# Two-layer trunk on one core: bulk work of GpSimd handed to VectorE and ScalarE, ALiBi slopes folded into the queries, the score products of two heads issued in turn, a product of the state-space part widened

## The chip, the cores and the metric

The kernel runs on one core of one Trainium2 chip. The metric is the device time of one execution in microseconds; the median of several executions counts. The engines are called as in the profile: PE (TensorE's matmuls), PEld (its weight loads), DVE (VectorE), ACT (ScalarE), POOL (GpSimd), SP (SyncE, which here issues the loads of the weights).

## The reference, cut to what matters

A sequence of 256 tokens of width 1024, in float32, goes through two layers. Each layer is a mixer and a feed-forward part. The mixer of layer 0 is a state-space mixer (S5, 48 groups of 16 channels, 64 states each), that of layer 1 is causal attention of 12 heads with ALiBi; beside both runs an attention of 4 heads into 256 memory tokens.

```python
for i in range(2):
    h = rmsnorm(x, g)
    z = h @ w_in[i]                       # the mixer's input and the memory queries
    mixed = s5(z[..., :768]) if i == 0 else moba(q, k, v, slopes)
    mem = softmax(mq @ mk.T / 8) @ mv     # 4 heads of 64, 256 memory tokens
    x = x + concat(mixed, mem) @ w_out[i]
    h = rmsnorm(x, g_ffn)
    x = x + (silu(h @ w_gate) * (h @ w_up)) @ w_down

def s5(u):                                # a: complex decay, b, c: complex maps, one per group
    bu = einsum('bsgc,gpc->bsgp', u, b)
    xs = scan(xs * a + bu)                # over the 256 tokens
    y  = einsum(real(xs), c_re) - einsum(imag(xs), c_im) + d * u
    y  = gelu(y)
    return y * sigmoid(y @ w_glu + b_glu)

def moba(q, k, v, slopes):                # with 256 tokens: plain causal attention
    s = q @ k.T / 8 - slopes[h] * (t - t')     # masked where t' > t
    return softmax(s) @ v
```

## The kernel before

**Products.** PE multiplies in a reduced float32 type (fp32r), so each operand is split in two: `hi` is the value rounded to that type and `lo` is the rest. A product is three matmuls, hi·hi, hi·lo and lo·hi, in `mm3` (L192, L193, L194). Weights arrive by DMA as 128x1024 tiles `raw` (a ring of four buffers); `split_hi` (L150) makes `whi` on ACT and `split_lo` (L168) makes `wlo` on DVE or on POOL. A table of two letters for each weight tile (`ENGINES0`, `ENGINES1`) decides that: "ag" is ACT and POOL, "av" is ACT and DVE. In the feed-forward parts all are "av". Activations are split likewise (L272 on ACT, L273 on DVE).

**Order.** The mixers are written as named steps, and two lists (`ORDER0`, `ORDER1`) set the order in which the steps are issued; within one engine that order stays. In `ORDER1`, `s4` is the scores of head 4, `x4` its exponentials, `n4` the normalisation, `t4` the transposition, `h4` the hi and lo halves of the probabilities, `p4` the product with the values, `o4` the output; `qp2`, `kp2` are the projections of a pair of heads, `qe2`, `ke2` their evacuation and splitting, and `a4` the ALiBi bias. Heads 0 to 3 are the memory's, 4 to 15 the causal ones.

**State-space part.** The 48 groups are worked in six units of eight. For each unit, `s5_ab` (L587 to L589) and `s5_wo` (L599 to L601) form the matrices `AB` and `wo` out of products `tA` and `tB`, of which half are made on POOL (L588, L599); `s5_angles` makes angles, cosines, sines and the decay `dec` (L627, POOL); `s5_tm` (L641) multiplies `AB` and `wo`, 32 columns of `AB` at a time; the scan is L691; `s5_turn` (L695 on POOL, L696 on DVE) turns the scan's result `Z` by the angles, and L704 to L706 multiply it out. Beside it stand the memory's keys and values: their row norms go through Newton steps on 128x2 tiles (L236 to L242), `diag` (L250), and the value tile `mv` (L298 on ACT, L299 on DVE), from which PE goes on at L190.

**Attention.** `alibi` (L958) makes `sb = -slope * dist` on POOL. `h_scores` multiplies a head's queries and keys, which sit on 64 of PE's 128 rows, an even head on the lower and an odd one on the upper half (L351 for the block that is partly masked, L192 to L194 for the other); all matmuls of a head are issued together. `h_exp` adds the scores to `sb` and takes the maximum (L364 on DVE, from PSUM and SBUF), negates it (L366) and exponentiates (L370 on ACT). `h_norm` takes the reciprocal of the sum (L376) and multiplies the probabilities by it (L378 on DVE, twice a head, from SBUF to SBUF).

Of the kernel before, what the change touches and what calls it, by code (L numbers as in the profile page):

```python
# [89 lines left out]
class Trunk:  # L90
# [29 lines left out]
    def plan(self, name, idx, shape, eng="av"):  # L120

        self.chunks.append((name, idx, shape, eng))

    def load_w(self, n=1, parts=1, between=None):
        for _ in range(n):
            if self.n_load < self.stop:
                name, idx, (a, b), eng = self.chunks[self.n_load]
# [8 lines left out]
                self.loaded.append((raw, b, eng))  # L136

    def split_hi(self):
        nc = self.nc
# [4 lines left out]
        raw, b, eng = self.loaded.pop(0)
        if eng == "":
            self.half.append((raw, None, b, eng))
            return
# [1 line left out]
        if eng[0] == "a":
            nc.scalar.activation(out=hi, in_=raw, func=AF.Copy)  # L150
        else:
            nc.gpsimd.tensor_scalar(hi, raw, 1.0, 0.0, op0=ALU.mult, op1=ALU.add)
        self.half.append((raw, hi, b, eng))

    def split_lo(self):
# [4 lines left out]
        raw, hi, b, eng = self.half.pop(0)  # L160
# [141 lines left out]
    def qk_evac(self, pool, ps, r, nm, bufs, keep=False):  # L302
# [14 lines left out]
    def mem_heads(self, out):  # L317
        hs = []
        for pr in range(2):
            for e in range(2):  # L320
# [3 lines left out]
                hs.append(h)  # L324
        return hs

    def moba_heads(self, p, q, k, vt, out):
        hs = []
        for e in range(2):
# [3 lines left out]
            hs.append(h)  # L333
        return hs

    def h_scores(self, h):
# [4 lines left out]
        h.s = s = self.bank("sc")  # L341
        if h.slope is None:
            h.blocks = [(0, slice(0, T)), (1, slice(T, 2 * T))]
            h.order, h.n0 = [0, 2, 1, 3], 0
            for i, c in h.blocks:
                t = slice(i * P, (i + 1) * P)
                self.mm3(s[:, c], [(qh[r, t], ql[r, t])], [(kh[r], kl[r])])
        else:
            h.blocks = [(0, slice(0, P)), (1, slice(P, P + T))]
            h.order, h.n0 = [0, 1, 2], P  # L350
            mm(s[:, 0:P], qf[r, 0:P], kf[r, 0:P], start=True, stop=True)  # L351
            self.mm3(s[:, P:P + T], [(qh[r, P:T], ql[r, P:T])], [(kh[r], kl[r])])
# [985 lines left out]
```

## Time and profile before

| | |
|---|---|
| executions | 646.88, 647.16, 649.87 us; median 647.16 us |
| profiled execution | 649.4 us, span 647.6 us |
| mean granted clock of TensorE in it | 0.978 of full speed |
| busy in the span | PE 95%, PEld 90%, DVE 71%, ACT 56%, POOL 15% |
| DMA | mean 163 GB/s, 105.8 MB |

The span runs from the first to the last instruction of the profiled execution; 1.8 us of its time lie outside. PE counts as busy while a matmul is under way, at whatever clock, so a busy PE is not yet one that could not be faster.

### The profile page before, as it was taken

The page shows a single profiled execution, that of the slowest core. Times are in us where ns is not written, and L with a number is a line of the kernel's source. Part 1 is how long each engine was busy: PE and PEld are TensorE (multiplying, and loading weights), DVE is VectorE, ACT ScalarE, POOL GpSimd, SP SyncE. Part 2 cuts the span into 40 slices and gives each one's busy share as a digit, 9 for nine tenths or more (in the row PEclk, how much of TensorE's full clock was granted, in tenths as well). Part 3 has the DMA queues.
Part 4 walks back from the last instruction along what each step waited for, and adds up shares of the span by engine and source line. Part 5 has one row for each costly group of instructions (what it writes and reads, how often), then busy time and mean ns, then how long its engine had stood idle before and what let it go on. Part 6 is the DMA issues. An engine that isn't in the chain of part 4 may idle for free. (4 is left out here: it accounts for less than half of the span.)

```text
span 647.6 us, 12327 instructions
## 1 busy us (share of the span) xinstructions
PE 615.9 (95%) x4808; PEld 585.3 (90%) x4808; DVE 462.0 (71%) x858; ACT 364.0 (56%) x651; POOL 94.0 (15%) x76
## 2 busy tenths in 40 slices
PE   6998889899999999999999999989999999999995
PEld 6877769789999999999999899979999999998884
DVE  7979767679766666666646999978776666664444
ACT  7584826668555555554444758746655555553333
POOL 2435531110000000000036522211000000000001
PEclk9999979899999999999999999979999999999998
DMA  7564231445655565556665334425555655555511
GB/s 216 173 192 117 66 97 50 155 172 185 206 194 192 194 191 193 190 189 182 203 196 184 124 106 156 131 97 167 194 193 192 194 193 194 193 177 181 187 55 66
DMA packets 35578, 105.82 MB, mean 163 GB/s; under 512 B 4032, under 2 KB 9280, under 8 KB 35520
## 3 DMA queue, kind: packets, MB, share of 16 engines
q1 hardware_dynamic: 35520, 105.03, 50.3%
q8 instruction: 38, 0.62, 0.4%
q14 instruction: 20, 0.16, 0.1%
HBM read 102.40 MB, written 1.05 MB: 160 GB/s over the span
## 5 line engine op out<-in xcount | busy, mean ns | idle before, releaser
L150 ACT ACTIVATE whi<-raw 128x1024 fp32r<-128x1024 f32 (+2 forms) x176 | 183.3, 1043 | 151.9 <-PE mm L193 105.6
L168 DVE TENSOR_TENSOR wlo<-raw,whi 128x1024 fp32r<-128x1024 f32 (+1 forms) x157 | 190.0, 1210 | 49.2 <-PE mm L1119 28.3
L168 POOL TENSOR_TENSOR wlo<-raw,whi 128x1024 fp32r<-128x1024 f32 (+2 forms) x19 | 44.8, 2363 | 240.7 <-PE mm L194 208.6
L1057 DVE TENSOR_TENSOR gu<-mm,rr 128x512 f32<-128x512 f32 x44 | 30.4, 692 | 51.4 <-PE mm L194 50.7
L192 PE MATMUL mm<-hh,whi 128*128 128x256 f32 x176 | 48.6, 276 | 0.0
L193 PE MATMUL mm<-hl,whi 128*128 128x256 f32 x176 | 48.6, 276 | 0.0
L194 PE MATMUL mm<-hh,wlo 128*128 128x256 f32 x176 | 48.6, 276 | 0.0
L272 ACT ACTIVATE hh<-ev 128x256 fp32r<-128x256 f32 x44 | 18.3, 419 | 36.7 <-DVE ev L1049 36.7
L192 PEld LDWEIGHTS mm<-hh,whi 128*128 128x128 f32 x176 | 33.0, 188 | 0.0
L193 PEld LDWEIGHTS mm<-hl,whi 128*128 128x128 f32 x176 | 33.0, 188 | 0.0
L194 PEld LDWEIGHTS mm<-hh,wlo 128*128 128x128 f32 x176 | 33.0, 188 | 0.0
L273 DVE TENSOR_TENSOR hl<-ev,hh 128x256 fp32r<-128x256 f32 x44 | 18.7, 425 | 19.7 <-ACT hh L272 19.6
L1146 POOL TENSOR_TENSOR o<-xt,gf 128x256 f32<-128x256 f32 (+1 forms) x3 | 2.8, 921 | 196.7 <-issue 193.3
L192 PE MATMUL mm<-xg0h,whi 128*128 128x256 f32 x102 | 29.8, 292 | 0.0
L193 PE MATMUL mm<-xg7l,whi 128*128 128x256 f32 x102 | 28.4, 278 | 1.1 <-DVE xg7l L268 1.1
L192 PE MATMUL mm<-xg7h,whi 128*128 128x256 f32 x102 | 28.3, 277 | 0.0
L193 PE MATMUL mm<-xg0l,whi 128*128 128x256 f32 x102 | 28.2, 277 | 0.0
L192 PE MATMUL mm<-xg1h,whi 128*128 128x256 f32 x102 | 28.2, 277 | 0.0
L194 PE MATMUL mm<-xg0h,wlo 128*128 128x256 f32 x102 | 28.2, 277 | 0.0
L194 PE MATMUL mm<-xg1h,wlo 128*128 128x256 f32 x102 | 28.2, 277 | 0.0
L193 PE MATMUL mm<-xg1l,whi 128*128 128x256 f32 x102 | 28.2, 276 | 0.0
L192 PE MATMUL mm<-xg2h,whi 128*128 128x256 f32 x102 | 28.2, 276 | 0.0
(429 smaller groups left out, 2188.8 us busy)
## 6 DMA issues: line engine op xcount, KB each, us to landing
raw<-in_w_gu SPq DMA_DIRECT2D x88, 512.0 KB, 3.7
raw<-in_w_down SPq DMA_DIRECT2D x30, 512.0 KB, 3.3
raw<-in_w_qkv SPq DMA_DIRECT2D x18, 512.0 KB, 3.4
raw<-in_w_out SPq DMA_DIRECT2D x16, 512.0 KB, 3.3
raw<-in_w_down SPq DMA_DIRECT2D x16, 448.0 KB, 3.2
raw<-in_w_u SPq DMA_DIRECT2D x5, 512.0 KB, 4.9
raw<-in_w_q SPq DMA_DIRECT2D x4, 512.0 KB, 4.0
wx<-wo SPq DMA_DIRECT2D x12, 128.0 KB, 3.0
```

Source lines behind the costliest of these rows:

```text
L150: nc.scalar.activation(out=hi, in_=raw, func=AF.Copy)
L168: e.tensor_sub(out=lo, in0=raw, in1=f32(hi))
L192: mm(out, ah, bh, start=(first and i == 0), stop=False)
L193: mm(out, ah, bl, start=False, stop=False)
L194: mm(out, al, bh, start=False, stop=(last and i == n - 1))
L272: self.nc.scalar.activation(out=h, in_=x, func=AF.Copy)
L273: self.nc.vector.tensor_sub(out=l, in0=x, in1=f32(h))
L1057: v.tensor_mul(t, ps, rr.rearrange("p a b -> p (a b)"))
L1146: (nc.gpsimd if i else v).tensor_mul(o[n][:, c], r, gf[:, a:b])
```

## The change

`ENGINES0` and `ENGINES1` are gone: every weight is split by ACT (`whi`) and DVE (`wlo`). Of the state-space part, the halves of `tA` and `tB` that POOL made, the product with the sines in `s5_turn` and the table `dm` go to DVE, and `dec` to ACT. The step `alibi` and its places in `ORDER1` are gone: the queries of a head are divided by its slope as they are evacuated (a column `units` of 1/slope, L297 after), DVE's row then subtracts the distances themselves from the scores, and the slope comes back as the scale of the exponential and in the negated maximum. The normalisation of the probabilities goes from DVE to ACT. The matmuls of the scores of an even head and its odd neighbour are issued in turn, one of either, at the place of the even head's step. `s5_tm` multiplies 128 columns of `AB` instead of 32 (the further 96 give rows that nobody reads). `ORDER0` and the rest of `ORDER1` stay; no DMA is added.

```diff
 def split_lo(self):
-        e = self.nc.vector if eng[1] == "v" else self.nc.gpsimd
-        e.tensor_sub(out=lo, in0=raw, in1=f32(hi))
+        self.nc.vector.tensor_sub(out=lo, in0=raw, in1=f32(hi))
...
 def qk_evac(self, pool, ps, r, nm, bufs, keep=False, c=None):
-        self.nc.vector.tensor_mul(t, ps, r)
+        if c is None:
+            self.nc.vector.tensor_mul(t, ps, r)
+        else:
+            self.nc.vector.scalar_tensor_tensor(t, ps, c, r, op0=ALU.mult, op1=ALU.mult)
...
     def h_scores(self, h):
+        if h.e:
+            return
+        todo = [self.score_list(z) for z in (h, h.other)]
+        for pair in zip(*todo):
+            for out, a, b, first, last in pair:
+                self.nc.tensor.matmul(out, a, b, start=first, stop=last)
...
 def h_exp(self, h):
-                v.tensor_tensor_reduce(out=src[:, c], in0=src[:, c], in1=h.s[:, c], scale=1.0, scalar=-3e38,
-                                       op0=ALU.add, op1=ALU.max, accum_out=mx[:, i:i + 1])
-            v.tensor_scalar_mul(nm, mx, -1.0)
+                v.tensor_tensor_reduce(out=src[:, c], in0=h.s[:, c], in1=self.dist[:, c], scale=1.0, scalar=-3e38,
+                                       op0=ALU.subtract, op1=ALU.max, accum_out=mx[:, i:i + 1])
+            v.tensor_scalar_mul(nm, mx, -h.slope)
...
 def h_norm(self, h):
-            v.tensor_scalar_mul(h.p[:, c], h.p[:, c], ri[:, i:i + 1])
+            nc.scalar.activation(out=h.p[:, c], in_=h.p[:, c], func=AF.Copy, scale=ri[:, i:i + 1])
...
 def s5_ab(self, b):
-            g.tensor_mul(at(m2, gg), be(u.b[1]), co(self.PI))
+            v.tensor_mul(at(m2, gg), be(u.b[1]), co(self.PI))
 def s5_wo(self, b):
-        g.tensor_mul(gic(m1), ce(u.c[0]), cw(self.WR))
+        v.tensor_mul(gic(m1), ce(u.c[0]), cw(self.WR))
...
-        nc.gpsimd.tensor_scalar(u.dec..., self.m4..., 1.0, 0.0, op0=ALU.mult, op1=ALU.add)
+        nc.scalar.activation(out=u.dec..., in_=self.m4..., func=AF.Copy)
 def s5_tm(self, b):
-            nc.tensor.matmul(ps[0:32, q * P:(q + 1) * P], u.AB[:, q * 160:q * 160 + 32],
+            nc.tensor.matmul(ps[:, q * P:(q + 1) * P], u.AB[:, q * 160:q * 160 + P],
 def s5_turn(self, b):
-        self.nc.gpsimd.tensor_mul(u.rs, u.z, u.rs)
+        self.nc.vector.tensor_mul(u.rs, u.z, u.rs)
```

**DVE where the memory's values are made.** These are rows of VectorE's instruction order in the state-space part, around `mv`; `rc`, `rs`, `tA`, `tB`, `wo` and `AB` are tiles of a unit, `rc_mem` the memory's row norms, `con` and `dm` constants. Before:

```order
L250 TENSOR_SCALAR diag<-con,rc_mem 128x128 x2
L691 SCALAR_TENSOR_TENSOR Z<-dec_343,vin_345 128x512
L601 TENSOR_TENSOR wo<-tA,tB 128x512
L696 TENSOR_TENSOR rc<-Z,rc 128x512
L603 TENSOR_TENSOR rc<-st_147,con 128x512
L587 TENSOR_TENSOR tA<-b_672,st_142 128x20x16
L606 TENSOR_SCALAR rs<-rc 128x512
L587 TENSOR_TENSOR tA<-b_672,st_142 128x20x16
L607 TENSOR_TENSOR rc<-rc,rs 128x512
L589 TENSOR_TENSOR AB<-tA,tB 128x640
L299 SCALAR_TENSOR_TENSOR mv<-mm,rc_mem,mv 128x4x64
```

After, from the first of the same unit's rows on:

```order
L601 TENSOR_TENSOR rc<-st_160,con 128x512
L228 SCALAR_TENSOR_TENSOR rs_w<-rs_v,rs_w 128x2
L155 TENSOR_TENSOR wlo<-raw,whi 128x1024
L229 SCALAR_TENSOR_TENSOR rc_mem<-rs_w,rc_mem 128x2
L604 TENSOR_SCALAR rs<-rc 128x512
L237 TENSOR_SCALAR diag<-con,rc_mem 128x128 x2
L605 TENSOR_TENSOR rc<-rc,rs 128x512
L286 SCALAR_TENSOR_TENSOR mv<-mm,rc_mem,mv 128x4x64 x2
L642 TENSOR_TENSOR tp<-tp,dm 32x8x16
L693 TENSOR_TENSOR rs<-Z,rs 128x512
L694 TENSOR_TENSOR rc<-Z,rc 128x512
```

The row `wlo<-raw,whi` of the first gate weight has come in ahead of the last Newton row `rc_mem`, of `diag` and of `mv`; the two products `tA` and the sum `AB` have moved out of this place, and the turn's product `rs<-Z,rs` stands behind `mv`.

**DVE at the last pair of causal heads.** Rows of the same engine in layer 1 between the exponentials of heads 12 and 13 and the scores of the last pair; `kkf`, `qqf` are the evacuated keys and queries of that pair, `kkl`, `qql` their lo halves, `otile` and `gl` outputs of earlier heads. Before:

```order
L376 RECIPROCAL ri<-sm 128x2
L378 TENSOR_SCALAR p<-p,ri 128x128
L378 TENSOR_SCALAR p<-p,ri 128x256
L307 TENSOR_TENSOR kkf<-mm,rr 128x256
L376 RECIPROCAL ri<-sm 128x2
L378 TENSOR_SCALAR p<-p,ri 128x128
L378 TENSOR_SCALAR p<-p,ri 128x256
L409 TENSOR_TENSOR otile<-pv,ot 64x256
L273 TENSOR_TENSOR kkl<-kkf,kkh 128x256
L273 TENSOR_TENSOR gl_4213<-otile,gl_4213 128x256
L307 TENSOR_TENSOR qqf<-mm,rr_4340 128x256
L273 TENSOR_TENSOR qql<-qqf,qqh 128x256
```

After:

```order
L374 RECIPROCAL ri<-sm 128x2
L295 TENSOR_TENSOR kkf<-mm,rr 128x256
L374 RECIPROCAL ri<-sm 128x2
L155 TENSOR_TENSOR wlo<-raw,whi 128x1024
L407 TENSOR_TENSOR otile<-pv,ot 64x256
L260 TENSOR_TENSOR kkl<-kkf,kkh 128x256
L260 TENSOR_TENSOR gl_4226<-otile,gl_4226 128x256
L297 SCALAR_TENSOR_TENSOR qqf<-mm,units,rr_4351 128x256
L155 TENSOR_TENSOR wlo<-raw,whi 128x1024
L260 TENSOR_TENSOR qql<-qqf,qqh 128x256
```

The four rows `p<-p,ri` have left the engine and two rows `wlo<-raw,whi` have come in, one ahead of `kkl`, one ahead of `qql`.

**PE at the memory's scores of layer 1.** Rows of the order of TensorE's matmuls; `mk0` and `mq` are the memory's keys and queries, `xg7h`, `xg0h` the activations of the projections around. Before:

```order
L194 MATMUL mm<-xg7h,wlo 128x256
L192 MATMUL sc<-mk0h,mqh 128x256
L193 MATMUL sc<-mk0l,mqh 128x256
L194 MATMUL sc<-mk0h,mql 128x256
L192 MATMUL sc<-mk0h,mqh 128x256
L193 MATMUL sc<-mk0l,mqh 128x256
L194 MATMUL sc<-mk0h,mql 128x256
L192 MATMUL sc<-mk0h,mqh 128x256
```

After:

```order
L181 MATMUL mm<-xg7h,wlo 128x256
L335 MATMUL sc<-mk0h,mqh 128x256 x2
L335 MATMUL sc<-mk0l,mqh 128x256 x2
L335 MATMUL sc<-mk0h,mql 128x256 x2
L335 MATMUL sc<-mk0h,mqh 128x256 x2
```

A row of the difference names neither the half of PE's rows nor the head; where it reads `x2`, the first is the even head's and the second the odd one's, for the same block of the queries.

## Rows read from the trace of the kernel before

**Rows 1.** From the page: the row of TensorE's granted clock in 40 slices of 16.2 us (tenths of full speed, 9 is 90% or more).

```profile
PEclk9999979899999999999999999979999999999998
```

**Rows 2.** The span in stretches: start and end, length, then busy time and count of PE, PEld, DVE, ACT and POOL, the granted clock, the DMA share and GB/s. The state-space part lies in the first three, layer 0's gate and output in the third, the feed-forward part of layer 0 in the fourth, layer 1's attention from 340 on.

```profile
16.20:62.70 46.50, 41.92 (x251) 35.89 (x251) 40.67 (x75) 29.66 (x67) 20.69 (x18) 0.97 0.55 168
62.70:97.10 34.40, 28.73 (x139) 24.12 (x140) 26.16 (x52) 17.74 (x34) 15.75 (x11) 0.85 0.25 77
97.10:157.00 59.90, 55.85 (x444) 52.39 (x443) 46.37 (x82) 41.14 (x88) 7.72 (x4) 0.97 0.41 131
157.00:340.00 183.00, 183.00 (x1614) 182.95 (x1614) 122.05 (x176) 95.57 (x136) 4.93 (x2) 1.00 0.60 195
340.00:372.40 32.40, 31.20 (x248) 28.76 (x247) 25.38 (x45) 20.13 (x41) 20.62 (x12) 1.00 0.48 154
372.40:420.00 47.60, 47.38 (x408) 45.76 (x408) 44.05 (x133) 34.94 (x87) 10.68 (x13) 1.00 0.41 134
420.00:440.00 20.00, 17.14 (x123) 15.87 (x122) 13.64 (x38) 9.24 (x25) 4.26 (x3) 0.83 0.24 79
```

**Rows 3.** POOL's groups over the whole span: line, operation, output and inputs, count, busy time and mean of one in ns, then the idle time before them and what ended it.

```profile
L168 POOL TENSOR_TENSOR wlo<-raw,whi 128x1024 fp32r<-128x1024 f32 (+2 forms) x19 | 44.8, 2363 | 240.7 <-PE mm L194 208.6 <-issue 14.9 <-ACT whi L150 14.6
L588 POOL TENSOR_TENSOR tB<-b,st 128x320 f32<-128x320 f32 x12 | 12.5, 1062 | 10.1 <-DVE AB L589 5.8 <-DVE wo L601 2.2 <-DVE rc L242 2.0
L695 POOL TENSOR_TENSOR rs<-Z,rs 128x512 f32<-128x512 f32 x6 | 12.0, 2001 | 40.8 <-DVE Z L691 35.4 <-DVE yl L273 5.5
```

**Rows 4.** Timeline of the widest hole of PE, in the state-space part: start, duration, engine, line, operation, count, and in brackets the idle time of the engine before it with what ended it.

```profile
74.07 4.51 POOL L695 TENSOR_TENSOR rs<-Z,rs 128x512 f32<-128x512 f32 x1 [5.56 <-DVE Z L691]
74.42 0.68 DVE L696 TENSOR_TENSOR rc<-Z,rc 128x512 f32<-128x512 f32 x1
75.02 0.69 DVE L603 TENSOR_TENSOR rc<-st,con 128x512 f32<-128x512 f32 x1
...
76.36 0.49 DVE L587 TENSOR_TENSOR tA<-b,st 128x320 f32<-128x320 f32 x1
...
76.77 0.68 DVE L607 TENSOR_TENSOR rc<-rc,rs 128x512 f32<-128x512 f32 x1
...
79.12 1.48 POOL L588 TENSOR_TENSOR tB<-b,st 128x320 f32<-128x320 f32 x2
...
80.56 4.15 POOL L168 TENSOR_TENSOR wlo<-raw,whi 128x1024 fp32r<-128x1024 f32 x2
80.63 2.95 DVE L589 TENSOR_TENSOR AB<-tA,tB 128x640 f32<-128x640 f32 x1 [3.18 <-POOL tB L588]
...
84.03 0.79 PE L190 MATMUL mm<-ms,raw 128*128 128x256 f32 x1 [5.36 <-DVE mv L299]
```

**Rows 5.** Timeline of DVE in the stretch before it, cut to three places: the row with which a unit's products begin, a sum AB, and the turn that ends the stretch; and the matmul that waits for that turn.

```profile
19.36 1.07 DVE L242 SCALAR_TENSOR_TENSOR rc<-rs_w,rc 128x2 f32<-128x2 f32 x1
...
25.56 0.82 DVE L589 TENSOR_TENSOR AB<-tA,tB 128x640 f32<-128x640 f32 x1 [1.37 <-POOL tB L588]
...
61.00 1.72 DVE L696 TENSOR_TENSOR rc<-Z,rc 128x512 f32<-128x512 f32 x1
...
62.78 0.67 PE L705 MATMUL sc<-wo,rc 128*128 128x128 f32 x2 [2.77 <-DVE rc L696]
```

**Rows 6.** Timeline of the hole before the last pair of causal heads; columns as in rows 4.

```profile
418.63 2.94 DVE L378 TENSOR_SCALAR p<-p,ri 128x128 f32<-128x128 f32 x2
...
419.01 2.40 POOL L168 TENSOR_TENSOR wlo<-raw,whi 128x1024 fp32r<-128x1024 f32 x1
...
423.03 2.01 DVE L273 TENSOR_TENSOR kkl<-kkf,kkh 128x256 fp32r<-128x256 f32 x1
...
425.77 0.80 PE L351 MATMUL sc<-kkf,qqf 64*128 64x128 f32 x4 [2.83 <-DVE qqf L307]
```

**Rows 7.** DVE's groups between 335 and 455 us, each shape apart: count, busy time and mean in ns, idle time before.

```profile
L168 DVE TENSOR_TENSOR wlo<-raw,whi 128x1024 fp32r<-128x1024 f32 x16 | 20.8, 1298 | 0.7 <-PE mm L194 0.7
L378 DVE TENSOR_SCALAR p<-p,ri 128x256 f32<-128x256 f32 x20 | 14.8, 758 | 0.1
...
L364 DVE CUSTOM_DVE_ANT_0 sb<-sb,sc 128x256 f32<-128x256 f32 x12 | 5.0, 414 | 0.0
...
L273 DVE TENSOR_TENSOR qql<-qqf,qqh 128x256 fp32r<-128x256 f32 x6 | 2.5, 416 | 0.5 <-ACT qqh L272 0.5
```

**Rows 8.** ACT's groups of the same stretch, in the same columns.

```profile
L150 ACT ACTIVATE whi<-raw 128x1024 fp32r<-128x1024 f32 x32 | 33.5, 1053 | 14.4 <-PE mm L193 8.5 <-PE mm L194 2.8 <-POOL wlo L168 1.8
...
L272 ACT ACTIVATE qqh<-qqf 128x256 fp32r<-128x256 f32 x6 | 2.5, 411 | 4.4 <-DVE qqf L307 4.4
```

**Rows 9.** A normalisation in layer 0, at a moment when POOL does nothing: two instructions of 128x256.

```profile
99.48 0.62 DVE L378 TENSOR_SCALAR p<-p,ri 128x256 f32<-128x256 f32 x2
```

**Rows 10.** PE's timeline around the scores of a pair of causal heads: the first, the last, and the first matmul behind them.

```profile
383.70 0.59 PE L351 MATMUL sc<-kkf,qqf 64*128 64x128 f32 x3
...
384.48 0.28 PE L194 MATMUL sc<-kkh,qql 64*128 64x256 f32 x1
384.69 0.38 PE L192 MATMUL mm<-xg0h,whi 128*128 128x256 f32 x1
```

**Rows 11.** PE's timeline around the products of `s5_tm` (L641, 32 columns held) and beside them those of L677 (128 columns held).

```profile
43.42 1.06 PE L641 MATMUL tp<-wo,AB 128*32 128x128 f32 x8
44.41 0.71 PE L677 MATMUL sc<-u,wp 128*128 128x128 f32 x4
```

More of the change, by code (lines that the diff above doesn't have):

```diff
@@ L118, in bank, with plan @@
         return getattr(self, "ps_" + kind).tile([P, 512], F32, tag=kind, name=kind)
-    def plan(self, name, idx, shape, eng="av"):
-        self.chunks.append((name, idx, shape, eng))
+    def plan(self, name, idx, shape, split=True):
+        self.chunks.append((name, idx, shape, split))
     def load_w(self, n=1, parts=1, between=None):
@@ L143, in split_hi @@
             return
-        raw, b, eng = self.loaded.pop(0)
-        if eng == "":
-            self.half.append((raw, None, b, eng))
+        raw, b, split = self.loaded.pop(0)
+        if not split:
+            self.half.append((raw, None, b))
             return
         hi = self.whi.tile([P, raw.shape[1]], F32R, tag="whi", name="whi")
[L149 to L153, printed above, removed]
+        nc.scalar.activation(out=hi, in_=raw, func=AF.Copy)
+        self.half.append((raw, hi, b))
     def split_lo(self):
@@ L159, in split_lo @@
             return
-        raw, hi, b, eng = self.half.pop(0)
+        raw, hi, b = self.half.pop(0)
         if hi is None:
@@ L324, in mem_heads @@
                 hs.append(h)
+            hs[-2].other = hs[-1]
         return hs
@@ L341, in h_scores @@
         h.s = s = self.bank("sc")
+        three = lambda c, t: [(s[:, c], a[r, t], b[r], i == 0, i == 2)
+                              for i, (a, b) in enumerate(((qh, kh), (qh, kl), (ql, kh)))]
         if h.slope is None:
@@ L344, in h_scores @@
             h.order, h.n0 = [0, 2, 1, 3], 0
[L345 to L352, printed above, removed]
+            return [m for i, c in h.blocks for m in three(c, slice(i * P, (i + 1) * P))]
+        h.blocks = [(0, slice(0, P)), (1, slice(P, P + T))]
+        h.order, h.n0 = [0, 1, 2], P
+        return [(s[:, 0:P], qf[r, 0:P], kf[r, 0:P], True, True)] + three(h.blocks[1][1], slice(P, T))
     def h_exp(self, h):
@@ L745, in glu, with plan0 @@
         v.scalar_tensor_tensor(l, w, 0.5, f32(h), op0=ALU.mult, op1=ALU.subtract)
-    def plan0(self, order, engines):
+    def plan0(self, order):
         halfk, full = (KT // 2, T), (KT, P)
@@ L759, in plan0 @@
             at[f"gC{i}"] = ("w_gluC", i, (6, P))
-        engines = iter(engines)
         for name in order:
             if name in at:
-                self.plan(*at[name], next(engines) if name[0] == "g" else "")
+                self.plan(*at[name], name[0] == "g")
     def mixers0(self, memcat, order):
@@ L891, in mixers0, with plan1 @@
         return S.gl
-    def plan1(self, order, engines):
+    def plan1(self, order):
         at = {}
@@ L905, in plan1 @@
             at[f"w{k}"] = ("w_out1", k, (KT, P))
-        engines = iter(engines)
         for name in order:
             if name in at:
-                self.plan(*at[name], next(engines))
+                self.plan(*at[name])
     def mixers1(self, pool, xs, sums, cat, order):
@@ L963, in scores @@
             if h.slope is not None:
-                h.sb = S.w[f"sb{i}"]
+                h.sb = pool.tile([P, 384], F32, tag="sb", name="sb", bufs=3)
             self.h_scores(h)
@@ L1180, in run @@
         layer(0)
-        self.plan1(ORDER1, ENGINES1)
+        self.plan1(ORDER1)
         layer(1)
@@ L1189, in run @@
         self.ident = self.con[:, C_ID:C_ID + P]
+        self.units = self.cst.tile([P, HEADS // 2], F32, name="units")
+        for n in range(HEADS):
+            nc.gpsimd.memset(self.units[64 * (n % 2):64 * (n % 2) + 64, n // 2:n // 2 + 1], 1.0 / SLOPES[n])
         memcat = self.hl("mcat", 2)
```

48 lines of the change are left out of this document (18 added, 30 removed).

## The prediction

> **What bounds the kernel now.** I read the table of stretches first, because PE's mean of 95% hides two kinds of stretch. In the feed-forward part PE never stops: 1614 matmuls fill 183.00 us, 0.113 us each, at clock 1.00, and POOL has next to nothing to do [rows 2]. The change touches nothing there, nor in the second such part, so what it is worth lies in the mixers. There PE is idle or slow in places: 4.6 of 46.5 us without a matmul between 16.2 and 62.7, 5.7 of 34.4 behind it, and 2.9 of 20 between 420 and 440 [rows 2]. The clock is lower in two of these stretches (0.85 and 0.83), the same dips as the 7s and 8s in the clock's row of the page [rows 1].
>
> Next I read what ends the holes. All three name DVE: the turn `rc` (2.77 us), the value tile `mv` (5.36 us), the queries `qqf` (2.83 us) [rows 4 to 6]. DVE is the busiest engine beside PE there (40.67 of 46.5 us, 44.05 of 47.6) [rows 2]. But its rows are not all honest work. The sum AB takes 2.95 us while POOL makes `wlo`, and 0.82 us otherwise [rows 4, 5]. Two products `p` take 2.94 us while POOL works, 0.62 otherwise [rows 6, 9], and over layer 1 the 128x256 ones average 758 ns [rows 7]. `kkl` takes 2.01 us; `qql`, the same shape, averages 416 ns [rows 6, 7]. A Newton row on 128x2 takes 1.07 us, the turn 1.72 against 0.68 [rows 4, 5]. The long `p` end at 421.6, POOL's `wlo` beside them at 421.4 [rows 6]. It can fall on the other side: while POOL's turn `rs` takes 4.51 us, DVE's rows from 74.42 on keep their pace [rows 4], and POOL's average 2001 ns [rows 3]. The rows that read PSUM do not stretch: `sb` from the scores keeps a mean of 414 ns with POOL's rows all around [rows 7]. So POOL's work, slow in itself (`wlo` 2363 ns against 1298 on DVE [rows 3, 7]), also holds DVE up, and at three places PE waits for DVE.
>
> **The change, part by part.** Each stretch is priced by what PE could do in it.
>
> *16.2 to 62.7.* DVE starts this stretch's work at 19.36 and ends the turn at 62.72, 43.4 us [rows 5]. In the changed order the same work, with POOL's share, is 71 rows: 31 of 512 (or 504) elements at 0.60 us (one start to the next), 20 of 320 at 0.41, 5 sums AB at 0.82 [rows 4, 5], two scans and 13 short rows, some 6 us by estimate: 18.6 + 8.2 + 4.1 + 6 = 37 us. DVE would end 6.5 us earlier if nothing else held it; it waits for PE and ACT too, so the gain lies between the hole of 2.77 us and 6.5. I take **4**.
>
> *62.7 to 97.1.* The hole before `mv` goes 5.36 → about 1.4: PE was ready at 78.67, and in the new order AB and its wait (3.18 + 2.95 us [rows 4]) are no longer ahead of `mv`, but a `wlo` of 1.3 us is, which itself waits for ACT's `whi`; `mv` then lands near 80. That is 4 us. Clock 0.85 over 34.4 us costs up to 5.2 us [rows 2], and the slow spells follow the holes; I take 4 back. Together **8**, bounds 3 (the hole half closed, the clock unchanged) and 10.6 (hole and clock both whole).
>
> *97 to 157.* PE lacks 4 us and 0.03 of the clock (1.8 us); POOL works 7.7 us there [rows 2]. I take **2**, bounds 0 and 5.8.
>
> *340 to 372.4.* 248 matmuls at 0.113 are 28.0 of 32.4 us [rows 2]. POOL is busy 20.6 of it. The chain from the row norms to the first scores is partly DVE's, partly PE's: **2**, bounds 0 and 4.4.
>
> *372.4 to 440.* 408 matmuls make 46.1 of 47.6 us, 123 make 13.9 of 20: 7.6 us of room, of which the hole is 2.83 and the clock of 0.83 costs 3.4 [rows 2, 6]. From 418.63 DVE needs 7.1 us until PE starts [rows 6]; without the four `p` and with a `wlo` of 1.3 us ahead of `qqf`, and the rest at 0.41 a row [rows 7], it is about 3.7. The hole closes by more than its length. I take **5**, bounds 0 and 7.6.
>
> *Scores in turn.* A causal pair takes 0.99 us, of which 0.21 is the change back to 128 rows [rows 10]. Eight matmuls one after the other would be 0.90 + 0.21, so neighbours already overlap a little. Fully side by side they would be 0.45 + 0.21, 0.33 less: 2.0 us for six pairs; the memory's four pairs, of twelve matmuls, would give 0.68 each, 2.7 by the same sum. Bounds 0 and 4.7; I take **2**, nearer the row that shows overlap already there.
>
> *Widened products.* Eight with 32 columns take 0.99 us, start to start, 0.124 each, and their neighbours with 128 columns run at the same pace [rows 11]. If the change of shape is what costs 0.01 each, 48 give **0.5**; bounds 0 and 1.2 (one change of 0.2 us for each unit [rows 10]). The Trainium skill, "TensorE: Matmul & The Clock Gate", section "LDWEIGHTS (loading the stationary operand)", has a load's time grow with its columns: 96 more would be 80 ns, 3.8 us dearer over 48 products if nothing hid the load (an estimate from that page). By that the term would be -3.8 and the total 4.3 us later; the pace of the 128-column rows speaks against it.
>
> *What is added.* Fifteen `wlo` in layer 1 and four in layer 0 cost DVE 1.3 us each, 25 us [rows 3, 7], 24 products in the state-space part 0.41 to 0.60 each, 13 us; the stretches lost and the norms gone (14.8 us for the 256-wide ones in layer 1 alone [rows 7]) about balance that. PE covers it, as long as the row behind is not what PE waits for. On ACT each head's normalisation costs about 0.41 + 0.30 (from 411 ns for 256 elements [rows 8]), 16 us over all heads, and it stands behind whatever ACT has queued, `whi` of 1053 ns above all [rows 8]; in `ORDER1` two or three steps of projections, some 2.7 us each by 24 matmuls, lie between a head's normalisation and its transposition, except in the last pairs. I charge **-2**, bounds 0 and -8.
>
> Sum: 4 + 8 + 2 + 2 + 5 + 2 + 0.5 - 2 = 21.5 us. The profiled execution took 649.4 us and would take 628; it stands 2.2 above the median of 647.2, on whose scale I forecast 626.
>
> **Rivals.**
> *DVE or ACT becomes the bound.* DVE was at 93% between 372 and 420, ACT at 73% [rows 2]. With ten heads' normalisations ACT goes from 34.9 to about 42 of 46, close to PE. Then layer 1 gives 0 to 2 instead of 7 and the gluA `wlo` keeps `mv` late: a gain of 4 to 13, 634 to 643.9. The Trainium skill, "VectorE: DVE Perf Modes", section "The perf-mode tier table (the rule you actually need)", gives VectorE double rate on such a product from SBUF, which speaks against moving it; the trace agrees, with 0.62 us for two on DVE [rows 9] and 0.82 at ACT's 411 ns [rows 8]. The rival's chance is 22%.
>
> *More.* All holes close, the clock stays up, the pairs run side by side: 6.5 + 10.6 + 4 + 4.4 + 7.6 + 4.7 = 38 us at the most, so 609 to 616. 16%.
>
> *No change.* The stretched rows would be slow for a reason of their own and only happen beside POOL's; the clean 0.62 and 0.82 at POOL's idle moments speak against. Within 0.5%, 643.9 to 650.4, which is about what a measurement of this kernel can tell from no change. 8%.
>
> *Slower.* Normalisation on ACT makes each head go ACT, DVE, ACT, PE. If PE waits for it in every head of layer 1 behind one `whi`, that is 1.05 + 0.7 = 1.75 us, 16 times, 28 us: 653. It decides above 1.35 us a head, where it eats the 21.5. For it speaks only that ACT's order is fixed; the steps between speak against. 6%.
>
> **How the numbers follow.** Forecast 616 to 634: 48%. With the rivals, faster by over 0.5% has 0.86, within 0.5% 0.08, slower 0.06. The range 608 to 643 leaves out the last two (14%), the last microsecond of the half gain and holes that close by more than their rows show, some 18% in all.
>
> **What would show it.** POOL's total should fall to a few us; AB near 0.8, `kkl` near 0.42, the turn near 0.68, Newton rows near 0.16; the three holes of 2.77, 5.36 and 2.83 gone or under 1.5, and the clock above 0.9 in those stretches; the feed-forward parts unchanged at 0.113 us a matmul; the causal pair at 0.7 to 0.9 us. Wrong would be: new holes of PE that name ACT's `p` or a `wlo` that waits for its DMA or for `whi`, with DVE's or ACT's queue full ahead of the row that PE needs.

## The result, and the profile after

The changed kernel takes 626.77 us (623.62 to 630.39, 4 runs) where the kernel before took 648.51 (646.88 to 650.37, 4 runs): a ratio of 0.967, 95% interval 0.960 to 0.973. The forecast was 626 within 608 to 643. The profiled execution of the changed kernel took 623.62 us, its span is 621.8 against 647.6. It is the fastest of the four; a_again, below, is the same kernel in an execution of 626.64 us.

The page of the changed kernel, its busy times and the row of the clock:

```profile
PE 603.6 (97%) x4808; PEld 576.4 (93%) x4808; DVE 446.8 (72%) x862; ACT 380.3 (61%) x697; POOL 5.7 (1%) x26
...
PEclk9999999999999999999999999999999999999998
```

POOL's 15% are 1%, and the dips of the clock in [rows 1] are gone but for the end. DVE took over 19 lo halves (some 23 us, at 1.2 us each) and 13 us of products, gave 40 rows of normalisation to ACT, and its total fell from 462.0 to 446.8 us. With those rows back on DVE (a_norm, below) it is 455.8 us for 902 rows, still less than before for 858.

The span of the changed kernel in stretches cut at the matmuls of the same numbers, in PE's order, as those of [rows 2]; columns as there:

```profile
15.70:55.80 40.10, 39.87 (x252) 35.46 (x252) 35.41 (x82) 30.58 (x69) 0.00 (x0) 1.00 0.61 190
55.80:79.00 23.20, 22.96 (x142) 19.89 (x140) 22.49 (x53) 18.01 (x36) 0.00 (x0) 1.00 0.30 91
79.00:136.90 57.90, 54.22 (x447) 50.93 (x444) 49.77 (x93) 46.01 (x99) 0.00 (x0) 1.00 0.47 150
136.90:319.90 183.00, 183.00 (x1615) 182.95 (x1614) 123.46 (x178) 95.68 (x136) 0.00 (x0) 1.00 0.61 195
319.90:349.40 29.50, 29.50 (x249) 27.99 (x248) 21.72 (x47) 21.04 (x47) 0.00 (x0) 1.00 0.51 165
349.40:397.70 48.30, 47.45 (x411) 45.18 (x408) 40.51 (x118) 41.63 (x107) 0.00 (x0) 1.00 0.40 132
397.70:414.70 17.00, 15.53 (x124) 14.06 (x123) 10.20 (x30) 11.92 (x33) 0.00 (x0) 1.00 0.28 93
```

The lengths against those before: 6.4 us less, 11.2 less, 2.0 less, none in the feed-forward part, 2.9 less, 0.7 more, 3.0 less. `ORDER0` and `ORDER1` alone do not fix the order to which a kernel compiles: `ORDER0` is unchanged, but at 352 of PE's first 885 places stands another matmul than before. So the bounds 55.80 and 79.00 cut the work at other points than 62.70 and 97.10, and only the first three stretches together are the same work: 19.6 us less (140.8 to 121.2), in a_again 17.6 less (123.3). Layer 1's attention, from 340 to 460, takes 5.0 us less, in a_again 4.0. In the second stretch PE is busy nearly throughout and the clock is 1.00 instead of 0.85. In the sixth ACT has become as busy as DVE (41.63 and 40.51 us).

DVE's groups of the changed kernel between 315 and 430 us, as [rows 7]:

```profile
L155 DVE TENSOR_TENSOR wlo<-raw,whi 128x1024 fp32r<-128x1024 f32 x31 | 37.6, 1218 | 4.3 <-PE mm L181 3.5 <-PE mm L180 0.8
...
L260 DVE TENSOR_TENSOR kkl<-kkf,kkh 128x256 fp32r<-128x256 f32 x6 | 2.5, 422 | 0.3 <-ACT kkh L259 0.3
```

`kkl` has the 0.42 us that `qql` had; `wlo` went from 1298 to 1218 ns. ACT's new groups in that stretch cost more than the prediction's 0.41 and 0.30 us:

```profile
L376 ACT ACTIVATE p<-p,ri 128x256 f32<-128x256 f32 x20 | 9.5, 497 | 0.6 <-DVE ri L374 0.6
...
L376 ACT ACTIVATE p<-p,ri 128x128 f32<-128x128 f32 x12 | 4.7, 392 | 0.7 <-DVE ri L374 0.7
```

The hole before the last pair of causal heads, [rows 6], is 1.24 us now:

```profile
397.35 1.48 ACT L376 ACTIVATE p<-p,ri 128x128 f32<-128x128 f32 x4
...
398.85 0.38 ACT L406 ACTIVATE ot<-pv 64x256 f32<-64x256 f32 x1
399.26 0.42 DVE L407 TENSOR_TENSOR otile<-pv,ot 64x256 f32<-64x256 f32 x1 [0.50 <-ACT ot L406]
...
400.96 0.42 DVE L260 TENSOR_TENSOR gl<-otile,gl 128x256 fp32r<-128x256 f32 x1 [0.82 <-ACT gl L259]
401.30 0.48 DVE L297 SCALAR_TENSOR_TENSOR qqf<-mm,units,rr 128x256 f32<-128x256 f32 x1
...
401.83 0.49 PE L335 MATMUL sc<-kkf,qqf 64*128 64x128 f32 x4 [1.24 <-DVE qqf L297]
```

Four normalisations in a row on ACT stand ahead of `ot`, which DVE's `otile` waits for (0.50 us). DVE's `gl` waits again (0.82 us) for its hi half on ACT, and `qqf`, which PE needs, is queued behind both.

### The profile page after: what moved, and what is told of

Read it like the earlier page. It is cut to its first block, busy times and chain, and to the rows that moved or that the text cites. A ratio compares the mean times of both kernels' runs of the same rounds, so it can differ in the third digit from the quotient of the medians.

```text
span 621.8 us, 12245 instructions
## 1 busy us (share of the span) xinstructions
PE 603.6 (97%) x4808; PEld 576.4 (93%) x4808; DVE 446.8 (72%) x862; ACT 380.3 (61%) x697; POOL 5.7 (1%) x26
## 4 chain that ended last, share of the span: by engine, by line
PE 82%; ACT 8%; DVE 8%; issue 1%; DMA 1%; SPq 0%; ACTq 0%; DVEq 0%
PE mm L179 20%; PE mm L180 20%; PE mm L181 20%; PE mm L177 4%; DVE wlo L155 2%; ACT p L368 2%; PE sc L1108 2%; PE sc L1109 2%; PE sc L1110 2%; PE sc L177 1%; PE tp L1110 1%; PE tp L1108 1%; PE tp L1109 1%; ACT whi L140 1%; PE pv L207 1%
## 5 line engine op out<-in xcount | busy, mean ns | idle before, releaser
L155 DVE TENSOR_TENSOR wlo<-raw,whi 128x1024 fp32r<-128x1024 f32 (+2 forms) x176 | 210.5, 1198 | 48.0 <-PE mm L1109 28.3
L180 PE MATMUL mm<-xg2l,whi 128*128 128x256 f32 x102 | 28.3, 277 | 0.0
L179 PE MATMUL mm<-xg3h,whi 128*128 128x256 f32 x102 | 28.3, 277 | 0.0
L181 PE MATMUL mm<-xg2h,wlo 128*128 128x256 f32 x102 | 28.2, 276 | 0.0
L181 PE MATMUL mm<-xg7h,wlo 128*128 128x256 f32 x102 | 28.2, 276 | 0.0
```

What stands on the lines that cost most here:

```text
L155: self.nc.vector.tensor_sub(out=lo, in0=raw, in1=f32(hi))
L179: mm(out, ah, bh, start=(first and i == 0), stop=False)
L180: mm(out, ah, bl, start=False, stop=False)
L181: mm(out, al, bh, start=False, stop=(last and i == n - 1))
```

## The experiments

Theory A: POOL's work held DVE up while both worked, whoever needed POOL's result. Rival B: POOL was only a slow maker of what others waited for. Beside them stands the question which parts of the change earned the gain. The table gives, for each run, the median and two times from its trace: when the matmul starts that stands at 157.06 us before (the end of layer 0's mixer), and how long PE takes from the matmul at 340.02 to that at 460.02 (layer 1's attention).

| kernel | median us | end of layer 0's mixer | layer 1's attention |
|---|---|---|---|
| before | 648.5 | 157.1 | 120.0 |
| changed | 626.8 | 136.9 | 115.0 |
| a_again (the changed one once more) | 625.5 | 139.0 | 116.0 |
| b_s5 | 637.1 | 142.5 | 122.8 |
| b_lo | 637.0 | 152.8 | 112.3 |
| b_both | 628.2 | 143.4 | 112.3 |
| a_norm | 626.4 | 142.0 | 111.8 |
| a_norm1 | 623.9 | 137.5 | 111.8 |
| a_norm1_again | 623.2 | 139.2 | 111.8 |
| a_unpair | 624.8 | 141.5 | 114.9 |
| a_norm1_unpair | 623.8 | 140.1 | 111.8 |
| a_busy | 661.1 | 174.2 | 115.0 |
| a_tied | 646.6 | 149.1 | 125.5 |
| a_tiedset | 626.3 | 138.8 | 116.1 |

Both times are from one execution each. a_unpair's starts 2 us late: its first product of the state-space part stands at 17.7 us, the others' (a_busy apart) at 15.7 to 16.3. The compiled order moves with the edit: in layer 0, PE's differs from that of the kernel before at 255 places in b_s5, 168 in b_lo and 357 in b_both, and from the changed kernel's at 77 in a_norm and 156 in a_unpair and a_norm1_unpair; a_norm1 keeps it there and differs in layer 1, at 72 places. Each of these runs measures its edit together with such a reordering. a_busy, a_tied and a_tiedset have the changed kernel's order on PE, DVE and ACT at every place.

**b_s5: only the state-space part's work moved.** The kernel before with the diff's lines of `s5_ab`, `s5_wo`, `s5_turn`, `dm` and `dec`:

```diff
-            g.tensor_mul(at(m2, gg), be(u.b[1]), co(self.PI))
+            v.tensor_mul(at(m2, gg), be(u.b[1]), co(self.PI))
...
-        self.nc.gpsimd.tensor_mul(u.rs, u.z, u.rs)
+        self.nc.vector.tensor_mul(u.rs, u.z, u.rs)
```

> The kernel before, with only the state-space part's bulk work moved (tB, tA, the turn's sines, dm to DVE, dec to ACT); POOL keeps the 19 lo halves and the ALiBi bias, all else stays. By the sum of the prediction the stretches up to 157 us gain 4 + 8 + 2, less what the gate's lo halves on POOL still cost there (1 to 3): 10 to 13 us, 635 to 639 against 648.5, and layer 1 keeps its holes. Rival (the lo half of the first gate weight on POOL is what makes the 5.36 us hole): the hole before mv stays at 3 us or more and the gain is 3 to 7 us, 641 to 646.

Measured: 637.06 us, ratio 0.981 (0.977 to 0.985). Layer 0's mixer ends 14.6 us earlier and no hole before `mv` is left, so the rival falls. Layer 1 is 2.8 us longer in this execution: there a DVE row of 128x2 came to run beside a lo half and took 2.42 us, and PE waited 2.7 us for the `diag` behind it.

**b_lo: only the lo halves moved.** The kernel before with another table:

```diff
-ENGINES0 = "ag ag av ag av ag"
+ENGINES0 = "av av av av av av"
```

and the 28 entries of `ENGINES1` likewise.

> The kernel before, with all lo halves of the weights on DVE (the table of engines reads av throughout); the state-space part and the ALiBi bias stay on POOL, the normalisation on DVE. Theory A: DVE's p, kkl and mql in layer 1 go back to 0.31 to 0.42 us, the 2.83 us hole goes and the state-space hole of 5.36 shrinks to 2 to 4: a gain of 5 to 9 us, 639 to 643. Rival (DVE becomes the bound): the 15 lo halves add 19 us to a DVE that was at 93% between 372 and 420, PE waits for DVE there and the time is 648 or more.

Measured: 637.01 us, ratio 0.980 (0.976 to 0.985), better than theory A's 639 and far from the rival. DVE's 128x256 `p` in layer 1 fell from 758 to 361 ns without being touched, `kkl` from 680 to 456. PE's hole before `mv` in this kernel:

```profile
83.19 7.13 PE L190 MATMUL mm<-ms,raw 128*128 128x256 f32 x24 [3.46 <-DVE mv L299]
```

3.46 us instead of the 5.36 of [rows 4], as expected: the lo half no longer stretches AB (0.83 us instead of 2.95), but AB still waits 3.18 us for POOL's `tB`.

**b_both: the two together.**

> The kernel before with the lo halves and the state-space part's work off POOL; the ALiBi bias stays on POOL, the normalisation on DVE, scores and products as before. b_s5 and b_lo each gained 12.5 us; if the two gains add up but for the part at the hole before mv, where both cut, 626 to 628, and slopes, normalisation, pairing and widening together are worth 0 to 1 us. If these four are worth the 3 to 5 us of the prediction's sum, 629 to 632.

Measured: 628.18 us, ratio 0.968 (0.964 to 0.973), between the two expectations. The gains of b_s5 and b_lo, 12.5 us each, give 20.6 together, 4.4 less than their sum; the hole before `mv`, where both cut, can be a part of that, and the rest is not shown. All else in the change (slopes, normalisation, pairs, widening) is worth the 1.4 us between 628.2 and 626.8, 2.7 by a_again, and the intervals overlap. Behind this small sum stand two larger ones: against a_again, layer 0 from 16.2 on takes 3.8 us more here and layer 1 takes 3.6 us less.

**a_busy: work on POOL that nobody reads.** The changed kernel with

```diff
+    def busy(self, src, n):
+        s = self.scr[:, :min(n, 512)]
+        self.nc.gpsimd.tensor_scalar(self.tick, src, 0.0, 1.0, op0=ALU.mult, op1=ALU.add)
+        for _ in range(max(1, n // 512)):
+            self.nc.gpsimd.tensor_mul(s, s, s)
```

called after each lo half that POOL had made, twice in `s5_ab` (on `u.b`), in `s5_wo` and in `s5_turn`.

> The changed kernel, with work given to POOL that nobody reads: at each of the 19 places where POOL made a `wlo` before, two products of 128x512 on a scratch tile, and for each unit of the state-space part four products (two of 320, two of 512 elements); a one-column copy ahead of each ties it to its place. The order of all other engines is that of the changed kernel. Theory A (POOL's work holds up DVE's whenever both use SBUF, whoever needs the result): DVE's rows that read two SBUF tensors stretch again (AB 0.8 to 1.2 us and more, kkl 0.42 to over 0.6), DVE's total rises by 10 to 25 us from 447, holes of PE that name DVE come back, and the time is 6 to 12 us above the changed kernel's 626.8, 633 to 639. Rival B (POOL was only a slow maker of what others waited for): nobody waits for this work, so DVE's rows stay and the time is within 0.5% of 626.8.

Measured: 661.07 us. It tells nothing between the theories: the products ran as soon as POOL was free, 22 of them from 4.40 us on without a break, none in layer 1, and the loads of `b`, with the loads queued behind them, had to wait for POOL's one-column copies. Layer 1, where no such product ran, kept its gain.

**a_tied: the same work at its place.** The one-column copy now writes into the scratch tile, so that the products follow it, and it reads `AB` instead of `b`:

```diff
-        self.nc.gpsimd.tensor_scalar(self.tick, src, 0.0, 1.0, op0=ALU.mult, op1=ALU.add)
+        self.nc.gpsimd.tensor_scalar(s[:, 0:1], src, 0.0, 1.0, op0=ALU.mult, op1=ALU.add)
```

> As a_busy, but each piece of idle POOL work starts with a copy into the scratch tile of one column of the tile it belongs to (whi, wo, AB, Z), so it can't run ahead of its place, and nothing ties it to a load: in a_busy most of it ran at the start and the loads of b waited for it. Orders of PE, DVE, ACT and SP as in the changed kernel. Theory A (POOL's work holds DVE up): in layer 1, where 15 lo halves' worth of POOL work runs, DVE's two-input rows stretch (kkl and gl from 0.42 to over 0.6 in the mean, wlo from 1.22 to over 1.35), and 2 to 4 of the 5 us that layer 1 gained are lost; over the whole kernel 4 to 12 us, 631 to 639. Rival B (POOL's slowness mattered as the maker of wlo, tA, tB and rs, its presence did not): layer 1 keeps its gain and the time is within 0.5% of 626.8.

Measured: 646.62 us (10 runs), ratio to the kernel before 0.997. Work whose result nobody uses takes back 20 of the 22 us, more than theory A's bound; rival B falls as the only cause. The page of a_tied:

```profile
PE 610.6 (95%) x4808; PEld 581.0 (90%) x4808; DVE 473.6 (73%) x862; ACT 381.2 (59%) x697; POOL 107.3 (17%) x129
```

DVE executes the same 862 instructions in 473.6 instead of 446.8 us. Real waits for POOL are small (DVE's AB 0.8 us, ACT's `whi` 1.7). The signs that theory A named for layer 1 mostly failed: from 340 to 450 us `kkl` and `gl` average 420 and 423 ns, as without POOL's work, and `wlo` 1284, short of 1350; of these lo halves `qql` alone rose clearly, from 421 to 562. The rows that read PSUM keep their time, `sb` 416 ns.

That the total comes so near to the kernel before is chance. From 16.2 to the end of layer 0's mixer a_tied takes 132.8 us, between the 140.8 before and a_again's 123.3; layer 1 takes 5.5 us more than before. So the run shows what POOL's presence can cost in this order, but it does not divide the 22 us among stretched rows, waits for POOL's slow results (AB's 3.18 us for `tB` in [rows 4]) and the new order. Where most of the 10 us lie by which layer 1 is longer than in the changed kernel, the chain of row norms on 128x2 tiles, DVE and POOL in a_tied:

```profile
340.68 0.96 DVE L236 SCALAR_TENSOR_TENSOR rs_w<-rs_v,rs_w 128x2 f32<-128x2 f32 x1
341.67 0.16 DVE L237 SCALAR_TENSOR_TENSOR rc<-rs_w,rc 128x2 f32<-128x2 f32 x1
341.87 0.89 DVE L235 TENSOR_TENSOR rs_w<-rc 128x2 f32<-128x2 f32 x1
...
343.18 0.97 DVE L235 TENSOR_TENSOR rs_w<-rc 128x2 f32<-128x2 f32 x1
344.08 1.21 DVE L161 TENSOR_TENSOR wlo<-raw,whi 128x1024 fp32r<-128x1024 f32 x1
345.21 0.99 DVE L236 SCALAR_TENSOR_TENSOR rs_w<-rs_v,rs_w 128x2 f32<-128x2 f32 x1
```

```profile
340.58 2.16 POOL L133 TENSOR_TENSOR scr<-scr 128x512 f32<-128x512 f32 x2
...
343.10 3.09 POOL L133 TENSOR_TENSOR scr<-scr 128x512 f32<-128x512 f32 x2
```

Each long row has two elements a partition and lasts about as long as one POOL product (1.04 us). The first long row ends at 341.64, when the first of POOL's two products from 340.58 ends. All four begin while a POOL product is under way. The `wlo` from 344.08 begins ahead of a product and is not held (1.21 us); POOL's two products from 343.10, the second of which begins at 344.22, take 3.09 us instead of 2.08. In the changed kernel the same rows are all short:

```profile
326.45 0.16 DVE L227 TENSOR_TENSOR rs_w<-rc 128x2 f32<-128x2 f32 x1
326.64 0.16 DVE L228 SCALAR_TENSOR_TENSOR rs_w<-rs_v,rs_w 128x2 f32<-128x2 f32 x1
```

PE in a_tied then waits for `diag`, and the clock, 1.00 up to 344 us, is 0.79 over these 16 us: 0.50 from 347 to 350, behind the wait, the lower of its two levels (1.2 and 2.4 GHz):

```profile
347.06 1.19 PE L247 MATMUL pv<-diag,ones 128*128 128x256 f32 x2 [2.90 <-DVE diag L245]
```

```profile
340.00:356.00 16.00, 13.10 (x90) 12.48 (x89) 13.06 (x24) 6.69 (x11) 9.86 (x12) 0.79 0.35 102
```

**a_tiedset: the same places, but POOL only writes.**

```diff
-            self.nc.gpsimd.tensor_mul(s, s, s)
+            self.nc.gpsimd.memset(s, 1.0)
+            self.nc.gpsimd.memset(s, 1.0)
```

> As a_tied, but each product of 128x512 on POOL (or of 320) is two memsets of the same tile, which write and read nothing; a memset of 512 took 0.54 us, so POOL is busy about as long. If it is reading of SBUF by both engines that holds DVE up, DVE's rows stay clean and the time is within 4 us of the changed kernel's 626.8. If any POOL work on SBUF holds it up, the Newton rows stretch to 0.5 us or more again and the time is 635 or more.

Measured: 626.27 us, that of the changed kernel. Its page:

```profile
PE 606.2 (97%) x4808; PEld 578.7 (93%) x4808; DVE 448.5 (72%) x862; ACT 380.4 (61%) x697; POOL 94.9 (15%) x188
```

POOL is as busy as before the change (94.9 us, then 94.0), and DVE takes 448.5 us. Of the 94.9 us, 58.2 are the memsets and 30.5 the one-column copies, which stay and read. The memsets write the tile twice where a product wrote it once. So it is not POOL's being busy, nor its writing, but its reading of whole tiles. The Trainium skill, "SBUF — State Buffer", section "Who interferes with whom", says this: a DVE instruction with two SBUF inputs contends with a GpSimd instruction that reads SBUF, not with one that only writes. These two runs agree, 473.6 against 448.5 us of DVE.

One kind of row is still held by the writes. Two rows with one SBUF input, whose clean time is 0.17 us, in the same chain of a_tiedset:

```profile
327.96 0.62 DVE L233 TENSOR_SCALAR rs_w<-rs_v 128x2 int32<-128x2 int32 x1
328.61 0.55 DVE L234 TENSOR_SCALAR rc<-rs_w 128x2 int32<-128x2 int32 x1
329.19 0.16 DVE L236 TENSOR_TENSOR rs_w<-rc 128x2 f32<-128x2 f32 x1
329.39 0.16 DVE L237 SCALAR_TENSOR_TENSOR rs_w<-rs_v,rs_w 128x2 f32<-128x2 f32 x1
```

```profile
328.03 0.53 POOL L133 MEMSET scr<- 128x512 f32 x1
328.61 0.52 POOL L134 MEMSET scr<- 128x512 f32 x1
329.19 0.53 POOL L133 MEMSET scr<- 128x512 f32 x1
```

Each lasts to the end of a memset (the first two), the first though it began 0.07 us ahead of it; the two-input rows behind them, with memsets still running, do not.

**a_norm: the normalisation back on DVE.** The changed kernel with

```diff
-            nc.scalar.activation(out=h.p[:, c], in_=h.p[:, c], func=AF.Copy, scale=ri[:, i:i + 1])
+            v.tensor_scalar_mul(h.p[:, c], h.p[:, c], ri[:, i:i + 1])
```

> The changed kernel with the normalisation of the probabilities back on DVE (two rows of 0.2 to 0.31 us a head now that POOL is silent), nothing else changed. If DVE is the scarcer engine there, its 40.5 us in the 48.3 us of the causal heads become 46.5 and PE waits for it: 627 to 631. Rival (ACT is the scarcer one since the change: 41.6 of 48.3 us, four normalisations of 1.48 us ahead of the evacuations that the last pair waits for): ACT loses 14 us, the hole of 1.24 us before the last pair closes and the time is 623 to 626.

Measured: 626.37 us, ratio 0.965 (0.961 to 0.969); neither side by time. But the table shows two effects of opposite sign: layer 1's attention is 3 to 4 us shorter, layer 0's mixer ends 3 us later than in a_again (2.7 by its length from 16.2 on).

**a_norm1: ACT in layer 0, DVE in layer 1.**

```diff
-            nc.scalar.activation(out=h.p[:, c], in_=h.p[:, c], func=AF.Copy, scale=ri[:, i:i + 1])
+            if self.layer1:
+                v.tensor_scalar_mul(h.p[:, c], h.p[:, c], ri[:, i:i + 1])
+            else:
+                nc.scalar.activation(out=h.p[:, c], in_=h.p[:, c], func=AF.Copy, scale=ri[:, i:i + 1])
```

> The changed kernel with the normalisation on ACT in layer 0 (the memory's four heads) and back on DVE in layer 1. Against the changed kernel a_norm gained 3.3 us in layer 1 by the matching matmuls and lost 3 us between 97 and 157, so both together should give 623 to 624, 3 us below the changed kernel. Rival (those differences are chance of the one profiled execution): 626 to 627.

Measured: 623.89 us, ratio 0.963 (0.958 to 0.968). Once more beside the changed kernel on one chip:

> The changed kernel once more, as the measure for a_norm1_again on the same chip: 624 to 629 us.

> a_norm1 once more, beside the changed kernel on one chip. If normalising layer 1's probabilities on DVE is worth what the matching matmuls say (layer 1 gains 8.3 us against 5.0), it is 2.5 to 3.5 us under a_again. Rival (chance of single executions): within 1 us of a_again.

Measured: 623.21 us (622.41 to 623.97, 5 runs), ratio 0.960 (0.958 to 0.963), against 625.52 (623.45 to 626.64, 5 runs), ratio 0.963 (0.960 to 0.966). The median is 2.3 us lower, just short of the 2.5 expected; the intervals still overlap, the layer 1 times of every trace (111.8 against 115.0 to 116.0) do not. In a_norm1 the hole before the last pair, and the stretch between the matmuls of the numbers that bound the sixth stretch above, are

```profile
399.90 0.49 PE L335 MATMUL sc<-kkf,qqf 64*128 64x128 f32 x4 [0.50 <-DVE qqf L297]
```

```profile
350.06:396.64 46.58, 46.43 (x412) 44.82 (x408) 43.88 (x138) 35.00 (x88) 0.00 (x0) 1.00 0.42 137
```

DVE is at 94% there and ACT at 75%, and the stretch is some 1.8 us shorter than with ACT at 86% and DVE at 84%. The share of busy time alone would have chosen the other way.

**a_unpair: the scores head by head again.** The changed kernel with `h_scores` of the kernel before.

> The changed kernel with the scores issued head by head as before. A causal pair takes 0.78 us in the changed kernel's trace (360.68 to 361.46) against 0.99 before, the memory's first pair 0.90 against 1.25: about 0.2 times six and 0.35 to 0.7 times four, 2 to 4 us, so 628.5 to 631. Rival (other work fills the same time, PE is not what ends layer 1's chain there): within 1 us of 626.8.

Measured: 624.78 us, ratio 0.965 (0.960 to 0.970). That is 2.0 us under the 626.8 and 0.7 under a_again: the pairs' 2 to 4 us are not there, and the rival fits beside a_again, not beside the 626.8 that it names. The same on a_norm1:

> a_norm1 with the scores issued head by head as before. With the normalisation on ACT the pairing was worth nothing (a_unpair 624.8 against 626.8). If that was because the pair's four normalisations then came due on ACT at once, the pairing should show here, with ACT freed of them: 1 to 3 us above a_norm1's 623.2 to 623.9. Rival (PE has slack at the scores whoever normalises): within 0.7 us of it.

Measured: 623.80 us (6 runs), ratio 0.961 (0.957 to 0.964), again the rival: layer 1 takes 111.8 us either way. A pair is shorter in the changed kernel:

```profile
360.67 0.49 PE L335 MATMUL sc<-kkf,qqf 64*128 64x128 f32 x4
...
361.46 0.39 PE L179 MATMUL mm<-xg0h,whi 128*128 128x256 f32 x1
```

0.79 us where [rows 10] have 0.99. But PE gives it back. In a_norm1_again it waits 0.50 us before the last pair, in a_norm1_unpair it doesn't (the other two waits in layer 1, 0.18 and 0.29 us, are the same in both). And the memory's second pair in layer 1 does not run side by side: its rows in a_norm1_again come in pieces, with other matmuls and a change of shape of some 0.2 us between them:

```profile
342.34 0.28 PE L181 MATMUL mm<-xg2h,wlo 128*128 128x256 f32 x1
342.55 0.38 PE L335 MATMUL sc<-mk1h,mqh 64*128 64x256 f32 x1
...
342.89 0.28 PE L335 MATMUL sc<-mk1h,mql 64*128 64x256 f32 x1
343.09 0.33 PE L384 MATMUL tp<-con,p 128*128 128x128 f32 x1
```

## Why the prediction was right, and where it was not

The time was right to a microsecond, and that is luck: the gain in layer 0 was forecast too small, the gain in layer 1 too large. The mechanism, DVE's rows stretched beside POOL's, was read from the trace before, and a_tied and a_tiedset show it by itself; how much of the 22 us it is, next to the waits for POOL's own results and the new order, they leave open.

*16.2 to 157.* Forecast 4 + 8 + 2 = 14 within 5.8 and 22.9; measured 19.6 in the profiled execution and 17.6 in a_again. 1.7 of the difference is the clock between 13 and 19 us, 1.00 in the first, 0.76 in a_again and 0.72 before. How the gain falls on the three terms can't be told, since the bounds cut the work at other points.

*The hole before `mv`.* The step that failed is "`mv` then lands near 80" and its hole of 1.4 us: there is no hole at all. The prediction took AB and its wait out of the work ahead of `mv`, put a `wlo` in, and left the rest of DVE's queue as it had stood. In the new order a unit's `wo` and its `rc` and the next turn have moved behind `mv` too: of the six units, DVE has made `wo` and AB for six ahead of `mv` before, for five now. From the end of the turn (62.72 before, 60.48 now) to `mv` pass 9.7 us instead of 20.8. Some 6 of the 11 us less are AB and its wait; the stretched rows give about 2, and the rest is the order (an estimate from DVE's rows):

```profile
70.16 0.88 DVE L286 SCALAR_TENSOR_TENSOR mv<-mm,rc_mem,mv 128x256 fp32r<-128x256 f32 x2
```

```profile
71.28 4.05 PE L177 MATMUL mm<-ms,raw 128*128 128x256 f32 x18
```

*340 to 372.4.* Forecast 2, measured 2.9, within its bounds.

*372.4 to 440.* Forecast 5, measured 2.3, in a_again 1.4. "The hole closes by more than its length" failed: 1.24 of 2.83 us remain. The queue of DVE was worked out as if every row's input were ready. The norms had only changed queue; on ACT they delay `ot`, and with it the rows behind. The clock's part came back whole in the profiled execution (1.00 instead of 0.83 in the last of these stretches) and in part in a_again (0.90), after the same hole of 1.24 and 1.23 us.

*What is added.* I charged -2 for the normalisation as a whole. It is about +3 in layer 0 (a_norm against a_again), and -3 to -4 in layer 1 (111.8 against 115.0 and 116.0). Its price on ACT was taken from a plain copy, 411 ns; with the column of factors it is 497 and 392 ns, 0.89 us a causal head instead of 0.71.

*Scores in turn.* Forecast 2, measured nothing by time; layer 0's mixer ends some 0.9 us later without it (140.1 against 139.2), layer 1 is the same. The term took each pair by itself, as if both heads were ready whenever the first was; a pair does get shorter (0.79 instead of 0.99 us), but the second memory pair of layer 1 runs in pieces, and before the last pair PE now waits for what it saved.

*Widened products.* Forecast 0.5. In the changed kernel eight of them take 0.90 us, start to start, against 0.99 in [rows 11]; six units would give 0.5, if all were issued like this one (three are, the others in pieces of two and six):

```profile
34.05 1.06 PE L639 MATMUL tp<-wo,AB 128*128 128x128 f32 x8
...
34.95 1.89 PE L177 MATMUL mm<-raw,xf 128*128 128x256 f32 x8
```

The 3.8 us of dearer loads do not show. Each load did become longer, by about the 80 ns that the prediction worked out, from 110 to 192 ns, but the loads run beside the products:

```profile
L641 PEld LDWEIGHTS tp<-wo,AB x48: 106/110/110, 36.8 to 110.9; 128*32 128x32 f32 x48
```

```profile
L639 PEld LDWEIGHTS tp<-wo,AB x48: 186/192/192, 33.9 to 95.7; 128*128 128x128 f32 x48
```

The first is the kernel before, the second the changed one (shortest, median and longest in ns). One reading of the prediction was off: the 8 in the clock's row [rows 1] stands at 113 to 129 us, in the stretch from 97 to 157, not in one of the two that it names.

Of the rivals, "no change" is refuted by a_tied and a_tiedset. "Slower" had the right place (ACT's queue) and a far too high price: about 3 us in layer 1, not 28. "DVE or ACT becomes the bound" was half right: ACT does hold up layer 1, but for 3 to 4 us and not for all that the change earns there. "More" stayed off: 1.24 us of the last hole remain, and the pairs gave nothing.

What stays open: b_s5's layer 1 was longer than before in one execution; how often its rows meet POOL's in that way was not tried. Nor was the kernel before run in the changed order, or the changed kernel in the order before.

## What to carry to other kernels

Before handing work to an idle engine, look at what it does to the rows of the others while it runs: in a_tied 107 us of POOL's work, for which the others hardly waited, cost 20 us by stretching DVE's rows. A row that is far longer than its twin of the same shape, and ends when another engine's row ends, is the sign to look for. Price a freed stall in the order to which the changed kernel compiles, row by row, and price a moved step in the queue that it joins: the same normalisation gained 3 us in one layer and lost as much in the other.

## What the runs showed of the hardware

A DVE instruction with two inputs on 128x2 elements took up to 0.99 us beside a POOL product that reads SBUF (2.42 us in b_s5, beside a `wlo` of 2.41) and 0.16 us beside a POOL memset. A DVE row with one SBUF input (0.17 us clean) took 0.55 and 0.62 us beside memsets too. The stretch is not in proportion to the size of DVE's row, which ends with POOL's. Where DVE's row began first, a `wlo` of 1.21 us, POOL's product was the one that was held (1.97 us instead of 1.04). The changed kernel's executions spread from 623.5 to 630.4 us. One source of it is the clock of the first microseconds, 1.00 in one execution and 0.76 in another between 13 and 19 us, after PE had waited 0.40 and 0.90 us; from 16 to 19 us it is 0.53 in the second, nearly all at the lower level, 1.2 of 2.4 GHz. Another is the clock behind the last hole of layer 1, 1.00 and 0.90.
